# A two-layer decoder trunk with a sparse mixture of experts: the loop over overflowing expert pieces moved in front of the first expert pair, the last pair joined by one-hot products

## The chip, the cores and the metric

The kernel runs on one core of a Trainium2 chip, in one launch. The metric is device time in microseconds (us), the median of repeated executions. The profile shows one execution, taken by the hardware profiler; its engines are PE (TensorE matmul; PEld is its weight load), DVE (VectorE), ACT (ScalarE), POOL (GpSimd) and SP (SyncE, which here only issues transfers; SPq is its queue of instructions).

## The reference, cut to what matters

512 tokens of width 1024 go through two layers. In each, attention of three kinds ends in an output projection and a layer norm; then a mixture of experts (4 groups of 8 experts, each token takes its best group and that group's two best experts) and a second layer norm. All is float32.

```python
for l in range(DEPTH):                                   # DEPTH = 2
    mix = hybrid_mixer(x, ...)
    x = layer_norm(DEEPNORM_ALPHA * x + mix, ln1_g[l], ln1_b[l])
    moe = hier_moe(x, ...)
    x = layer_norm(DEEPNORM_ALPHA * x + moe, ln2_g[l], ln2_b[l])

def hier_moe(t, ...):
    lg = t @ rg_w + rg_b                                 # 4 groups, best one taken
    le = ...                                             # its 8 experts, best two taken
    gate = ...                                           # (token, group, expert), two nonzero per token
    for g in range(N_GROUPS):                            # expert: 1024 -> 2 x 256 -> 1024
        h = silu(t @ w_gate[g]) * (t @ w_up[g])
        y = y + (h * gate[:, g]) @ w_down[g]
```

## The kernel before

**The expert stage.** After the output projection, the rows of a layer are normalized without gain and bias and stored to DRAM (`xd`). A router on DVE picks two experts for each token. Every expert has 64 slots (`CAP`); two experts form a pair, so one pair is a list of 128 token rows, and there are 16 pairs for each layer. `hots` and `lists` make the lists: a one-hot matrix of slots by comparison, then a small product that gives each slot's row number and weight. `fetch` (through `gathered`, L1000) has POOL gather a pair's 128 rows from `xd`; `turned` transposes them on PE (L1011) and applies gain and bias on the way out of PSUM (L1015, L1017); `experts_up` multiplies by the gate and up weights (tile `S`); `experts_mid` makes silu times up; `experts_down` transposes that (`hT`), multiplies by the down weights (tile `o`), scales the rows on ACT (L1044) and DVE (L1045), and POOL adds the 128 rows to the sum `y2` in DRAM (L1046) by an indirect transfer that accumulates.

**The sum in DRAM.** `y2` begins as the normalized rows with gain and bias: `first_rows` makes them on DVE (L888, L889) in place, once the store to `xd` has read the tile, and ACT's queue stores them. After the last pair, SP loads `y2` back (L1251), the second norm follows (L1260 to L1265), and the result goes to `out` in the last layer, or is transposed and multiplied by the next layer's projection in the first.

**The weights.** The weights of one expert are two tiles of 1.5 MB (6144 columns in all), a pair has four, a layer 64. `load_next` issues one unit, that is two tiles, into a ring of 13 rooms: `RING = "UUAAARTTXUUmm"`, where T and m lie in the pool of the expert stage, which opens when attention's pool closes, and X in `xroom`. Six units (12 tiles) are asked for before the first pair, and each pair asks for two more, so a room is filled again once the pair that read it is done with it. SP's queue issues them in order.

**Overflow.** An expert with more than 64 tokens has the rest cut into pieces of 64. `pieces` counts them on DVE and lists them; `overflow` is a loop on the chip (`For_i`, L1139) whose number of turns every engine loads from memory (L1138). It stands behind the last pair and in front of the loads of `y2`. A turn loads the expert's two tiles whole (L1143), finds the piece's rows (L1146 to L1187), and does a small expert as above, ending in an accumulating transfer (L1209). With these inputs the first layer's loop has no turn and the second layer's has one.

**The next layer's weights.** In the first layer, the first chunk of the next projection is loaded and split into high and low parts (`load_pair`, L196, L199) behind the last pair's work, by `issue_after` on the last instruction of each engine.

Each engine works through its instructions in the order in which the tile framework's planner wrote them; only the loop's borders and the `issue_after` marks are set by hand.

## Time and profile before

| | |
|---|---|
| median of 3 runs | 1386.83 us (1380.25 to 1387.82) |
| the profiled execution | 1385.0 us, span 1383.2 us |
| PE busy | 1194.4 us (86%) |
| PE weight loads | 815.8 us (59%) |
| DVE busy | 696.6 us (50%) |
| ACT busy | 442.9 us (32%) |
| POOL busy | 292.5 us (21%) |
| HBM | 278.06 MB read, 31.82 MB written |

The shares are averages over two layers with several stages each. The span has the first layer's attention until about 380 us, its experts until about 660 us, the second layer's attention until about 1045 us and its experts until the end. For the change only the two expert stages and their borders matter, so they are read stage by stage.

### The profile page before, as it was taken

The page shows a single profiled execution, that of the slowest core. Times are in us where ns is not written, and L with a number is a line of the kernel's source. Part 1 is how long each engine was busy: PE and PEld are TensorE (multiplying, and loading weights), DVE is VectorE, ACT ScalarE, POOL GpSimd, SP SyncE. Part 2 cuts the span into 40 slices and gives each one's busy share as a digit, 9 for nine tenths or more (in the row PEclk, how much of TensorE's full clock was granted, in tenths as well). Part 3 has the DMA queues.
Part 4 walks back from the last instruction along what each step waited for, and adds up shares of the span by engine and source line. Part 5 has one row for each costly group of instructions (what it writes and reads, how often), then busy time and mean ns, then how long its engine had stood idle before and what let it go on. Part 6 is the DMA issues. An engine that isn't in the chain of part 4 may idle for free. (4 is left out here: it accounts for less than half of the span.)

```text
span 1383.2 us, 18273 instructions
## 1 busy us (share of the span) xinstructions
PE 1194.4 (86%) x6701; PEld 815.8 (59%) x6708; DVE 696.6 (50%) x1822; ACT 442.9 (32%) x1050; POOL 292.5 (21%) x286
## 2 busy tenths in 40 slices
PE   6989999999939989887599999999996699898860
PEld 6989976668924533222398899666795343332320
DVE  7599638684552422111668892668636333211125
ACT  3362256673102221111235322857611122111100
POOL 5332431201001121100332334230000122111011
PEclk9999999999969999999799999999998799999985
DMA  7321440115397999998552224200426899999943
GB/s 240 116 80 51 128 158 11 36 40 185 118 402 279 400 413 405 409 390 287 166 165 78 65 83 140 98 23 22 156 104 247 347 384 407 409 403 410 356 166 123
DMA packets 63898, 293.81 MB, mean 212 GB/s; under 512 B 16064, under 2 KB 20672, under 8 KB 48192
## 3 DMA queue, kind: packets, MB, share of 16 engines
q1 hardware_dynamic: 52128, 267.43, 50.5%
q0 software_dynamic: 9376, 16.81, 4.9%
q10 hardware_dynamic: 2304, 8.39, 1.5%
q8 instruction: 54, 0.88, 0.3%
q14 instruction: 36, 0.29, 0.1%
HBM read 278.06 MB, written 31.82 MB: 224 GB/s over the span
## 5 line engine op out<-in xcount | busy, mean ns | idle before, releaser
L97 PE MATMUL acc<-U,xh 128*128 128x384 f32 (+1 forms) x1584 | 298.9, 343 | 18.9 <-DVE xh L212 7.0
L97 PEld LDWEIGHTS acc<-U,xh 128*128 128x128 f32 x1584 | 280.5, 193 | 21.9 <-issue 6.9
L97 PE MATMUL S<-w,xg 128*64 128x512 f32 (+1 forms) x968 | 272.0, 608 | 10.6 <-DMA w<-w_e 8.9
L97 PEld LDWEIGHTS S<-w,xg 128*64 128x64 f32 x968 | 83.1, 141 | 138.8 <-issue 112.9
L1017 DVE TENSOR_SCALAR xg<-acc,lv 128x128 f32<-128x128 f32 x128 | 45.8, 404 | 179.6 <-PE S L97 142.9
L97 PE MATMUL o<-w,hT 128*64 128x512 f32 x488 | 125.4, 603 | 5.9 <-ACT hT L90 3.4
L199 POOL TENSOR_TENSOR U<-raw,U 128x768 fp32r<-128x768 f32 (+2 forms) x46 | 90.3, 1967 | 166.9 <-ACT U L196 166.9
L1046 POOL DMA_INDIRECT y<-xroom,ri x32 | 51.4, 1607 | 294.8 <-DVE xroom L1045 180.5
L1031 ACT ACTIVATE h<-S 128x256 f32<-128x256 f32 x32 | 12.3, 383 | 270.6 <-PE S L97 270.6
L196 ACT ACTIVATE U<-raw 128x768 fp32r<-128x768 f32 (+2 forms) x88 | 68.0, 812 | 71.6 <-PE acc L97 43.7
L1045 DVE TENSOR_SCALAR xroom<-o,rv 128x512 f32<-128x512 f32 x32 | 24.0, 751 | 117.7 <-PE o L97 117.7
L97 PEld LDWEIGHTS o<-w,hT 128*64 128x64 f32 x488 | 39.2, 138 | 67.1 <-issue 57.4
L1000 POOL DMA_INDIRECT xroom<-xd,ri x33 | 35.2, 1066 | 180.5 <-PE acc L1011 94.5
L199 DVE TENSOR_TENSOR U<-raw,U 128x768 fp32r<-128x768 f32 (+2 forms) x42 | 52.8, 1260 | 36.5 <-ACT U L196 34.0
L1011 PEld LDWEIGHTS acc<-cst,xroom 128*128 128x128 f32 x256 | 29.4, 147 | 60.6 <-issue 36.0
L90 ACT ACTIVATE uc<-T 128x512 f32<-128x512 f32 (+3 forms) x117 | 51.3, 460 | 40.9 <-PE T L297 39.1
L1015 ACT ACTIVATE xg<-acc,lv 128x128 f32<-128x128 f32 x128 | 48.9, 458 | 45.5 <-PE T L97 35.8
L1011 PE MATMUL acc<-cst,xroom 128*128 128x128 f32 x256 | 43.7, 298 | 22.7 <-DMA xroom<-xd,ri 20.7
L97 PE MATMUL acc<-U,oh 128*128 128x384 f32 (+1 forms) x384 | 63.3, 315 | 0.0
L1044 ACT ACTIVATE xroom<-o,rv 128x512 f32<-128x512 f32 x32 | 22.0, 687 | 111.0 <-PE o L97 111.0
L97 PEld LDWEIGHTS acc<-U,oh 128*128 128x128 f32 x384 | 56.8, 189 | 1.2 <-issue 1.0
L403 DVE MATCH_REPLACE8 uc<-m,uc 128x256 f32<-128x256 f32 (+2 forms) x96 | 51.4, 539 | 0.0
(367 smaller groups left out, 1942.0 us busy)
## 6 DMA issues: line engine op xcount, KB each, us to landing
w<-w_e SPq DMA_DIRECT2D x110, 1536.0 KB
raw<-w_in SPq DMA_DIRECT2D x64, 384.0 KB
xroom<-w_e SPq DMA_DIRECT2D x8, 1536.0 KB
w<-w_e SPq DMA_DIRECT2D x24, 512.0 KB
raw<-w_o SPq DMA_DIRECT2D x16, 384.0 KB
gb<-ln_rows SPq DMA_DIRECT2D x4, 1024.0 KB
xd<-yn ACTq DMA_DIRECT2D x8, 512.0 KB
y<-yn ACTq DMA_DIRECT2D x6, 512.0 KB
```

The lines of the kernel that those rows point to most:

```text
L90: A.activation(o, i, AF.Copy, scale=1.0 if scale is None else scale)
L97: return PE.matmul(o, l, r, start=start, stop=stop, skip_group_check=True)
L196: A.activation(hi, r, AF.Copy)
L199: e.tensor_tensor(lo, r, hi.bitcast(F32), OP.subtract)
L403: V.match_replace(out=acc_t[i][:, :n], in_to_replace=m8, in_values=acc_t[i][:, :n], imm_value=TAKEN)
L1000: G.indirect_dma_start(out=xr[0:n], out_offset=None, in_=xd, in_offset=bass.IndirectOffsetOnAxis(ap=ri[0:n], axis=0), bounds_check=S - 1, ...
L1011: PE.transpose(t[:, 128 * j:128 * j + 128], xr[:, 128 * k:128 * k + 128], ident)
L1015: A.activation(xg[:, k], o, AF.Identity, scale=lv[:, 0, k, 0:1], bias=lv[:, 0, k, 1:2])
L1017: V.tensor_scalar(xg[:, k], o, lv[:, 0, k, 0:1], lv[:, 0, k, 1:2], op0=OP.mult, op1=OP.add)
L1044: last_on["A"] = A.activation(y[:, 0:512], o[0], AF.Copy, scale=rows[1])
L1045: last_on["V"] = V.tensor_scalar(y[:, 512:1024], o[1], rows[1], None, op0=OP.mult)
L1046: return G.indirect_dma_start(out=y2, out_offset=bass.IndirectOffsetOnAxis(ap=rows[0], axis=0), in_=y, in_offset=None, bounds_check=S - 1, ...
```

## The change

- **`y2` begins at zero**, stored early in the layer from a zeroed slot of 512 columns; `first_rows` is gone. In its place each pair adds half of the normalized row with gain and bias to its own rows (each token stands in two lists): `gb1` is halved once by ACT, `half_rows` makes the row on DVE from the gathered rows, and the rows are taken out of PSUM by two `scalar_tensor_tensor` on DVE, which add it. ACT takes no part in that any more. The copy of `hT` is always DVE's.
- **Rooms.** Gathered rows and output rows are tiles of the expert stage's pool; `xroom` holds two rooms of the ring and four small rooms of 512 columns (256 KB). The ring is `UUAAARTTXXUUm`, again 13.
- **`pieces` and `overflow` stand in front of the first pair**, behind the fetch of pairs 0 and 1 and six units of weights. A turn loads its weights in 12 parts of 512 columns through the four small rooms, in front of the products that read them.
- **The last pair** is not added to `y2`. `sums` loads the second norm's gain and bias and `y2` (which then holds all other pairs) before the last pair's work; the last list's one-hot matrix is transposed (`pT`), and a product of it with the last pair's rows gives their share per token in PSUM. In the last layer a product with the identity adds `y2` in PSUM; in the first layer DVE adds it.
- **The next layer's first chunk** is loaded and split during the last pair, behind `h`, with DVE alone for the low part.

```diff
-            units = {"n": 0, "m": None}
+            units = {"n": 0, "X": 0, "m": None}
...
-                    return xroom[:, 0:UNIT]
+                    units["X"] += 1
+                    return xroom[:, UNIT * (units["X"] % 2):UNIT * (units["X"] % 2) + UNIT]
...
-            RING = "UUAAARTTXUUmm"
+            RING = "UUAAARTTXXUUm"
...
+            y2 = dr.tile([S, D], F32, name="y2", tag="y2")
+            none = ring("P")
+            G.memset(none, 0.0)
+            SP.dma_start(y2.rearrange("(p r) c -> p (r c)", r=NT).rearrange("p (n c) -> p n c", c=512), none.unsqueeze(1).to_broadcast([128, 2 * NT, 512]))
...
-            def first_rows(i):
-
-                z = yn[i] if i < NT - 1 else at.tile([128, D], F32, name="x1", tag="u", bufs=3)
-                V.tensor_tensor(z, yn[i], gb1[:, 0], OP.mult)
-                V.tensor_tensor(z, z, gb1[:, 1], OP.add)
-                A.dma_start(y2[128 * i:128 * i + 128, :], z)
-
+            A.activation(gb1.rearrange("p a d -> p (a d)"), gb1.rearrange("p a d -> p (a d)"), AF.Copy, scale=0.5)
...
-                if i:
-                    first_rows(i - 1)
...
             def row_room():
-                turns["y"] += 1
-                return carve(xroom, UNIT + 2 * D + D * (turns["y"] % 3), [D])
-
-            def gathered(ri, n=128):
-
-                xr = carve(xroom, UNIT + D * (turns["x"] % 2), [D])
-                turns["x"] += 1
+                return mo.tile([128, D], F32, name="y", tag="y", bufs=3)
+
+            def gathered(ri, n=128, tag="xr", bufs=2):
+
+                xr = mo.tile([128, D], F32, name="xr", tag=tag, bufs=bufs)
...
+            def half_rows(xr, n=128):
+
+                y = row_room()
+                V.tensor_tensor(y[0:n], xr[0:n], gb1[0:n, 0], OP.mult)
+                V.tensor_tensor(y[0:n], y[0:n], gb1[0:n, 1], OP.add)
+                return y
+
+            def next_half(p1):
+                if p1 in XR:
+                    with tc.issue_after(last_on["h"].ins):
+                        HR[p1] = half_rows(XR.pop(p1))
+                    if p1 in ahead:
+                        fetch(ahead[p1])
...
-            def experts_down(h, w, rows):
+            def experts_down(h, w, rows, y, p1):
                 hT = cp.tile([128, 2, 128], F32, name="hT", tag="rw")
-                transposes(hT.rearrange("p a b -> p (a b)"), [h[:, 0:128], h[:, 128:256]], 128)
+                transposes(hT.rearrange("p a b -> p (a b)"), [h[:, 0:128], h[:, 128:256]], 128, None, "V")
+                next_half(p1)
+                if w_next:
+                    w_next.pop()()
...
-                y = row_room()
-                last_on["A"] = A.activation(y[:, 0:512], o[0], AF.Copy, scale=rows[1])
-                last_on["V"] = V.tensor_scalar(y[:, 512:1024], o[1], rows[1], None, op0=OP.mult)
-                return G.indirect_dma_start(out=y2, out_offset=bass.IndirectOffsetOnAxis(ap=rows[0], axis=0), in_=y,
+                for n in range(2):
+                    c = slice(512 * n, 512 * n + 512)
+                    last_on["V"] = V.scalar_tensor_tensor(y[:, c], o[n], rows[1], y[:, c], op0=OP.mult, op1=OP.add)
+                return y
+
+            def added(y, ri, n=128):
+                return G.indirect_dma_start(out=y2, out_offset=bass.IndirectOffsetOnAxis(ap=ri[0:n], axis=0), in_=y[0:n],
                                             in_offset=None, bounds_check=S - 1, oob_is_err=False, compute_op=OP.add)
...
-            for p in range(2):
-                fetch(p)
-            first_rows(NT - 1)
             attn.__exit__(None, None, None)
...
-            load_next(3)
-            XG[0] = turned(XR.pop(0))
-            lists(1)
-            fetch(2)
-
+            for p in range(2):
+                fetch(p)
...
-                    w = [unit("T", "w") for _ in range(2)]
-                    for u in range(2):
-                        SP.dma_start(w[u], a["w_e"][l, bass.ds(er, 1), u].rearrange("o p f -> p (o f)"))
+                    n_part = [0]
+
+                    def part(u, c0):
+
+                        r = carve(xroom, 2 * UNIT + 512 * (n_part[0] % 4), [512])
+                        n_part[0] += 1
+                        SP.dma_start(r, a["w_e"][l, bass.ds(er, 1), u, :, c0:c0 + 512].rearrange("o p f -> p (o f)"))
+                        return r
...
                     for k in range(NK):
+                        wk = part(k // 6, 512 * (k % 6))
                         for h, c in enumerate(two):
-                            mm(gu[c, 0:FH], xg[:, k], gate_up(w, k)[:, FH * h:FH * h + FH], k == 0, k == NK - 1)
+                            mm(gu[c, 0:FH], xg[:, k], wk[:, FH * h:FH * h + FH], k == 0, k == NK - 1)
...
-            for p in range(NE // 2):
+            pieces()
+            load_next(3)
+            overflow()
+            XG[0], HR[0] = turned(XR[0]), half_rows(XR.pop(0))
+            lists(1)
+            fetch(2)
+
+            last, PL, w_next, yts = l == DEPTH - 1, NE // 2 - 1, [], []
...
+            def next_weights():
+                with tc.issue_after(last_on["h"].ins):
+                    Wc[l + 1, 0] = load_pair(w_in_src(l + 1, 0), chunks[0][1], "V")
+
+            def sums():
+
+                yus = [unit("A", "yt") for _ in range(2)]
+                for j in range(2):
+                    SP.dma_start(yus[j][:, 2 * D:3 * D], a["ln_rows"][l:l + 1, 1, j].to_broadcast([128, D]))
+                for j in range(2):
+                    yu = carve(yus[j], 0, [2, D])
+                    for i in range(2):
+                        yts.append(yu[:, i])
+                        r = 256 * j + 128 * i
+                        y2d = SP.dma_start(yu[:, i], y2[r:r + 128, :])
+                return [yu[:, 2 * D:3 * D] for yu in yus], y2d
...
+                if p == PL:
+                    gb2, y2d = sums()
...
+                elif not last:
+                    raw_room()
+                    w_next.append(next_weights)
...
+                if p == PL - 1:
+
+                    pT = mo.tile([128, NT, 128], F32, name="pT", tag="xr", bufs=2)
+                    transposes(pT.rearrange("p a b -> p (a b)"), [Pf[:, i, 128:256].bitcast(F32) for i in range(NT)], 128)
...
+                if p != PL:
+                    sts[p] = added(y, rows[0])
...
-            overflow()
...
+            for i in range(NT):
+                zb[i] = [bank(("acc", "S", "o")[i % 3]) for _ in halves]
+                for t, c in zip(zb[i], halves):
+                    if last:
+                        mm(t, ident, yts[i][:, c], True, False)
+                    mm(t, pT[:, i], y[:, c], not last, True)
...
-                src = [z[:, c] for c in halves]
+                src = [z[:, c] for c in halves] if not last else zb[i]
+                if not last:
+                    for t, c in zip(zb[i], halves):
+                        V.tensor_tensor(z[:, c], z[:, c], t, OP.add)
```

## Rows read from the trace of the kernel before

**Rows 1.** The chain that ended last, 1205 to 1317: start, us, what

```profile
1205.24 35.27 DMA w<-w_e
```

**Rows 2.** Windows, first layer: length, engines' busy us (instructions), PE clock, DMA share, GB/s

```profile
376.00:412.00 36.00, 15.03 (x94) 11.22 (x94) 21.55 (x87) 2.93 (x4) 3.34 (x3) 0.69 1.01 399
412.00:428.00 16.00, 13.79 (x58) 6.45 (x58) 5.43 (x23) 4.59 (x10) 1.99 (x2) 0.74 0.44 158
440.00:600.00 160.00, 145.00 (x659) 59.84 (x661) 44.99 (x159) 30.09 (x74) 29.61 (x23) 0.98 1.02 408
```

**Rows 3.** The same windows, second layer

```profile
1076.00:1092.00 16.00, 7.15 (x30) 5.79 (x32) 7.58 (x43) 2.30 (x5) 3.55 (x3) 0.50 1.02 431
1092.00:1100.00 8.00, 7.93 (x40) 2.96 (x38) 1.52 (x5) 1.30 (x4) 0.20 (x1) 0.96 0.44 139
1100.00:1317.00 217.00, 197.45 (x884) 73.79 (x880) 54.76 (x181) 39.15 (x96) 37.07 (x28) 0.98 1.00 395
```

**Rows 4.** Timeline of SP: the first weights into rooms that pair 0 freed

```profile
423.83 0.80 SPq L530 DMA_DIRECT2D w<-w_e  x2
...
1096.81 0.80 SPq L530 DMA_DIRECT2D w<-w_e  x2
```

**Rows 5.** Timeline: a first row that waits for its store, and pair 0's gather, both layers

```profile
387.66 1.23 DVE L888 TENSOR_TENSOR yn<-yn,gb 128x1024 f32<-128x1024 f32 x1 [4.74 <-DMA xd<-yn]
403.73 1.78 POOL L1000 DMA_INDIRECT xroom<-xd,ri  x1 [21.48 <-DVE ri L986]
...
1067.73 1.22 DVE L888 TENSOR_TENSOR yn<-yn,gb 128x1024 f32<-128x1024 f32 x1 [5.30 <-DMA xd<-yn]
1077.57 1.54 POOL L1000 DMA_INDIRECT xroom<-xd,ri  x1 [22.16 <-DVE ri L986]
```

**Rows 6.** Timeline of PE: pair 0's gathered rows turned, first up products

```profile
414.14 1.97 PE L1011 MATMUL acc<-cst,xroom 128*128 128x128 f32 x8 [6.67 <-DMA xroom<-xd,ri]
416.68 8.83 PE L97 MATMUL S<-w,xg 128*64 128x512 f32 x32
...
1090.22 8.29 PE L97 MATMUL S<-w,xg 128*64 128x512 f32 x32
```

**Rows 7.** Timeline of DVE: first and last of the 17 instructions of `pieces`

```profile
1138.33 0.38 DVE L1117 TENSOR_TENSOR over<-cnt,cst 128x224 f32<-128x224 f32 x1
...
1144.01 0.16 DVE L1132 TENSOR_SCALAR eidi<-eid 128x16 int32<-128x16 f32 x1
```

**Rows 8.** Timeline of the loop's one turn in the second layer

```profile
1329.85 0.23 DVE L1146 TENSOR_SCALAR h<-cst,ctr 128x16 f32<-128x16 f32 x1 [0.42 <-DVE xroom L1045]
1340.88 5.81 PE L97 MATMUL S<-w,xg 128*64 128x256 f32 x32 [1.51 <-DVE xg L1189]
1352.21 1.44 POOL L1209 DMA_INDIRECT y<-xroom,ri  x1 [15.64 <-DVE xroom L1208]
```

**Rows 9.** Tiles `xroom` and `y`, second layer's expert stage: issue to landing

```profile
DMA to landing us min/median/max: 2.6/10.1/12.0
...
DMA to landing us min/median/max: 9.1/11.2/12.0
```

**Rows 10.** Waits of SP around the loop in the first layer: us, times, longest

```profile
SPq L1139 <- DMA y<-xroom,ri: 11.2, 1, 11.2
```

**Rows 11.** Timeline: last pair's end and first statistics of the second norm, both layers

```profile
655.63 3.71 PE L97 MATMUL o<-w,hT 128*64 128x512 f32 x16 [0.56 <-issue]
668.92 0.06 DVE L1134 MEMSET ctr<- 128x1 f32 x1 [3.60 <-issue]
671.69 0.69 DVE L1260 BATCH_NORM_STATS2 bst<-yt 128x6 f32<-128x512 f32 x1 [2.71 <-DMA yt<-y]
...
1323.47 5.17 PE L97 MATMUL o<-w,hT 128*64 128x512 f32 x16 [0.52 <-ACT hT L90]
1328.68 0.75 DVE L1045 TENSOR_SCALAR xroom<-o,rv 128x512 f32<-128x512 f32 x1 [6.22 <-PE o L97]
1359.57 0.69 DVE L1260 BATCH_NORM_STATS2 bst<-yt 128x6 f32<-128x512 f32 x1 [7.63 <-DMA yt<-y]
```

More of the change, by code (lines that the diff above doesn't have):

```diff
@@ L956, in trunk @@
             V.tensor_scalar(hot, hot, TAKEN, None, op0=OP.is_equal)
-            selb = small.tile([128, NT, 8, 4], BF, name="selb", tag="selb", bufs=1)
+            selb = small.tile([128, NT, 8, 4], BF, name="selb", tag="stN", bufs=1)
             gb = ghot.unsqueeze(2).to_broadcast([128, NT, 8, 4])
@@ L1216, in trunk @@
                 h = experts_mid(gu)
-                if p + 1 < NE // 2:
-                    XG[p + 1] = turned(XR.pop(p + 1))
-                    fetch(p + 3)
-                if p % 2 == 0 and p // 2 + 2 < NE // 4:
-                    lists(p // 2 + 2)
-                st = experts_down(h, w, RI.pop(p))
-                load_next()
-                if p % 2:
-                    tc.declare_no_dep(st.ins, st0.ins, reason="a token has one group: the two pairs of a batch share no row")
-                st0 = st
-                if p == 3:
-                    pieces()
-                    gb2 = norm_rows(1)
-            last = l == DEPTH - 1
-            with tc.issue_after(last_on["PE"].ins), tc.issue_after(last_on["A"].ins), tc.issue_after(last_on["V"].ins), tc.issue_after(st.ins):
-                if not last:
-                    raw_room()
-                    Wc[l + 1, 0] = load_pair(w_in_src(l + 1, 0), chunks[0][1], "VG")
-            overflow()
+                if p != PL:
+                    p1 = ORDER[q + 1]
+                    with tc.issue_after(last_on["up"].ins):
+                        XG[p1] = turned(XR[p1])
+                elif not last:
+                    raw_room()
+                    w_next.append(next_weights)
+                if q + 4 < n:
+                    p4 = ORDER[q + 4]
+                    if p4 % 2 == 0:
+                        Pf = lists(p4 // 2)
+                if p == PL - 1:
+                    pT = mo.tile([128, NT, 128], F32, name="pT", tag="xr", bufs=2)
+                    transposes(pT.rearrange("p a b -> p (a b)"), [Pf[:, i, 128:256].bitcast(F32) for i in range(NT)], 128)
+                rows = RI.pop(p)
+                y = experts_down(h, w, rows, HR.pop(p), ORDER[q + 1] if p != PL else None)
+                load_next()
+                if p != PL:
+                    sts[p] = added(y, rows[0])
+                    if p < PL and p % 2:
+                        tc.declare_no_dep(sts[p].ins, sts[p - 1].ins, reason="a token has one group: the two pairs of a batch share no row")
             if not last:
-                warm(10)
                 XH[l + 1] = xhp.tile([128, 2, NK, S], F32R, name="xh", tag="xh")
@@ L1243, in trunk @@
             halves = [slice(0, 512), slice(512, 1024)]
-            yts = []
-            for j in range(2):
-                yu = carve(unit("A", "yt"), 0, [2, D])
-                for i in range(2):
-                    yts.append(yu[:, i])
-                    r = 256 * j + 128 * i
-                    for c in halves if r == 0 else [slice(0, 1024)]:
-                        y2d = SP.dma_start(yu[:, i, c], y2[r:r + 128, c])
-            if not last:
-                with tc.issue_after(y2d.ins):
-                    Wc[l + 1, 1] = load_pair(w_in_src(l + 1, 1), chunks[1][1], "VG")
+            zb = {}
+            for i in range(NT):
[4 more added lines that the diff above has]
+                    mm(t, pT[:, i], y[:, c], not last, True)
             for i in range(NT):
                 z = yts[i]
-                src = [z[:, c] for c in halves]
+                src = [z[:, c] for c in halves] if not last else zb[i]
+                if not last:
+                    for t, c in zip(zb[i], halves):
+                        V.tensor_tensor(z[:, c], z[:, c], t, OP.add)
                 st = small.tile([128, 2, 6], F32, name="bst", tag="bst", bufs=4)
```

49 lines of the change are left out of this document (27 added, 22 removed).

## The prediction

> **What bounds the kernel now.** I read the chain of waits first. In the second layer's expert stage it is a run of weight loads, four links from 1205 to 1317, the first of 35.27 us [rows 1]. The windows by stage say the same of both layers: the DMA share is 1.02 from 440 to 600 and 1.00 from 1100 to 1317, at some 400 GB/s [rows 2, 3]. So the expert stage ends when its transfers have gone through, and only time in which the transfers rest can be won or lost. They rest once in each layer, at the start: share 0.44 for 16 us (9.0 us idle) and 0.44 for 8 us (4.5 us) [rows 2, 3]. There all free rooms are filled, and SP waits for pair 0 to free the first: the refills at 423.83 and 1096.81 [rows 4] come 7.2 and 6.6 us after pair 0's first up product at 416.68 and 1090.22 [rows 6]. From there the transfers do not stop until the last pair. This is the rule for the sum: each microsecond by which pair 0 begins sooner or later moves the end of its layer's expert stage by one, and work on PE or DVE inside the stage costs nothing as long as it hides under the loads.
>
> What follows the last weights is bare: in the first layer 12.4 us from the last down product's end (655.63 + 3.71) to the first statistics at 671.69; in the second 30.9 us, from 1328.64 to 1359.57, with the loop's one turn in it [rows 11].
>
> **First layer, front.** The first rows go. DVE waited 4.74 us for the store to `xd` and then had four such instructions of 1.22 us between the router's own [rows 5], 9.6 us. Pair 0's gather moves from 403.73 to about 394, and with the 10.4 us that it took to reach PE [rows 5, 6] it lands at about 404.5. New in between: `pieces`, 17 instructions over 5.8 us [rows 7], behind the lists at about 395, so until 401; then the loop with no turn. What that costs shows at its old place: DVE stood 3.60 us before its next instruction at 668.92 [rows 11], and SP had waited 11.2 us there for a transfer [rows 10], so I read the exit as a meeting of all engines that also waits for transfers in flight. 401 + 3.6 gives 404.6. The weights asked for before would be in by about then: the transfers were full to 412 [rows 2] with one tile of 1.5 MB and 2 MB of first-row stores that now fall away, 3.5 MB at 399 GB/s, 9 us. So the loop ends at 406 to 408; PE needs 2.5 us from the first transposes to the first up product [rows 6], which then comes at 408.5 to 410.5. I take the later: 6 us won. Bounds: 9 if the loop is hidden by the gather; 3 if the jump takes as long as a gather under full load, 10.1 us [rows 9], ending at 411.
>
> A page of the Trainium skill speaks for the lower bound: Runtime: NRT & Kernel Launch, section Instruction fetch mechanics, says that a taken branch to a target outside the two blocks held makes the sequencer fetch it by DMA before it goes on. The trace agrees in that engines stand at the exit; no row separates fetch from meeting. By that rule the jump competes with full weight queues and the term is 3, not 6.
>
> **First layer, end.** The 12.4 us hold extraction, the accumulating transfer, the loop's exit and the load of `y2`. In their place: two extractions by DVE, 0.75 us each as its old one [rows 11]; two products of 512 columns (sixteen half-width ones took 3.71 us [rows 11], so 0.2 to 0.9 each, I take 0.9); two additions, 0.75 each as the extraction: 4.8 us. Then the split of the next layer's weights: it lay in the hidden wait, and that cover is gone. Four subtractions on DVE, at most 1.23 each [rows 5], either stand ahead of the extraction (and wait for their load, which SP issues only behind the reads of `y2`) or follow it: 0 to 5 us, I take 2.5. Won: 12.4 − 4.8 − 2.5 = 5, bounds 3 and 8.
>
> **Second layer, front.** Without the first rows DVE saves 5.30 + 4 × 1.22 = 10.2 us; but the gather needs the store to `xd`, which landed at 1067.73 [rows 5]: it starts at 1068, not 1077.57, and the lists are done at about 1068.5. `pieces` ends at 1074, the loop begins at about 1075 with room for a first move. Its turn took 22.4 us from first DVE work to its last transfer (1329.85 to 1352.21), 1.4 to issue that [rows 8] and 2.6 at least to land [rows 9]: 26.4. New in it: weights by parts. The up products took 5.81 us for eight parts' worth [rows 8], 0.73 a part; four parts are there at the start, the fifth is asked for after the first is read and is in 2.6 us later [rows 9], 0.4 late, and the four for the down product likewise. I take 3 us, bounds 1 and 6 (landing at 5). PE starts it at clock 0.50 [rows 3], having stood: I take 2, bounds 0 and 5.8, all up products at half speed. Extraction by DVE alone and the half rows have DVE idle beside them. Exit 1.5, bounds 1 and 3.6. So 1075 + 26.4 + 3 + 2 + 1.5 = 1108, first up product 2.5 later, 1110.4: 20 us lost. Bounds 14 and 30. The thirteenth tile (3.8 us at 408 GB/s) fits between exit and first refill.
>
> **Second layer, end.** The turn and the load of `y2` leave the tail. After 1328.64: 1.5 us extraction, 0.9 to 1.8 product (the identity product needs only `y2` and can go first). `y2` itself waits for the adding of pair 14, median 11.2 us to land [rows 9]; pairs come about 15 us apart at the end (four tiles of 3.8), so it lands near the last product's end and the read 2.6 later. I take 4 us to the first statistics, bounds 3 and 8: 27 won, bounds 23 and 28. The norm starts with a whole row at once, not halves: 0.5, bounds 0 and 1.5.
>
> **Inside the stage.** DVE gets 2 × 1.22 for half a row, 0.75 more extraction and each `hT`: some 3.4 us a pair, 51 on 54.76 busy of 217 [rows 3]. Cover: the weight loads; price if it fails, in the rivals. The zeroing of `y2` and ACT's halving lie under attention and the output projection, where transfers and ACT have room; nothing if so.
>
> **Sum**, against the profiled execution's 1385.0 (span 1383.2): 6 + 5 − 20 + 27 + 0.5 = 18.5 won, 1366.5. The median lies 1.8 above that execution: **1368 us**. All bad ends give 3 + 3 − 30 + 23 + 0 = −1, so 1388; all good ones 9 + 8 − 14 + 28 + 1.5 = 32.5, so 1354.
>
> **Rivals.**
> *The jump pays for its fetch* (the rule above): 3 us less in the first layer and the exit at 3.6 in the second: 1373. For it: 3.60 us idle; against: the second layer's exit lay between 1352.21 and 1359.57 with transfer and load inside.
> *The read of `y2` still gates the end*: POOL adds pair 14 late because it works in order behind the adding before; the read lands 8 us after the last product in both layers, so 23 and 1 instead of 27 and 5: 1376. For it: the 11.2 us landings; against: 15 us a pair.
> *DVE becomes a link of each pair, slower than before*: the two `o` banks are free only after the extraction, and that may stand behind the half rows. PE had 197.45 busy of 217 [rows 3], some 1.4 us of room in each of 14.5 pairs. If all 3.4 us enter the chain, 2.0 a pair over 28 pairs is 56: 1424. It decides from about 0.9 us a pair beyond the room. Against: between two down products lie up products of 8 us.
> *Parts one at a time, slower too*: if the rooms work as one, 12 × (2.6 + 0.73) = 40 us for 11 in my sum: 1397. Against: `xroom` already held gathered rows, output rows and weights at the same time. A rule of the Trainium skill (DMA: Bandwidth & Descriptors, section Bandwidth: batch transfers to at least 1 MiB) speaks against parts; no row shows a load that small.
> *Better than 1354*: the loop hides more than its bounds say.
>
> **How the numbers follow.** Chances: forecast 0.55 (own range 1357 to 1379), jump 0.14, `y2` 0.12, DVE 0.07, parts 0.06, better 0.06. The range 1354 to 1386 holds the first three nearly whole and leaves 0.18 out. A measurement here tells 0.5% (6.9 us) from no change. Faster: 0.51 + 0.13 + 0.09 + 0.06 = 0.79; same: 0.04 + 0.01 + 0.03 + 0.01 = 0.09; slower: 0.07 + 0.05 = 0.12.
>
> **What would show it.** In the changed kernel's profile: pair 0's gather some 10 us earlier in both layers; first up products at about 411 and 20 us later than before in the second layer; transfers resting there for some 30 us after 1080; share near 1.0 afterwards; statistics some 4 us behind the last down product. It is wrong if the share inside the stage falls below 0.95 (DVE rival), if the turn takes 45 us (parts), or if the idle at the loop is much longer than these numbers.

## The result, and the profile after

The changed kernel takes 1369.89 us (median of 4 runs, 1367.66 to 1371.29), the kernel before 1386.34: ratio 0.9893, 95% interval 0.9863 to 0.9923. The forecast was 1368. The profiled execution takes 1368.62 us, with a span of 1366.8.

The time falls into nine stages whose borders are rows of the timelines: the router's first group maximum (DVE, 382.76 and 1055.92 before, 382.99 and 1047.68 after), the first weights into rooms that pair 0 freed (SP, [rows 4] before), the end of the last pair's down product (PE) and the first statistics of the second norm (DVE, both [rows 11] before).

| stage | before | after | difference | foreseen |
|---|---|---|---|---|
| 1 start to the first layer's router | 382.8 | 383.0 | +0.2 | 0 |
| 2 router to first refill, first layer | 41.1 | 34.9 | -6.2 | -6 |
| 3 first refill to last down product | 235.5 | 239.8 | **+4.3** | 0 |
| 4 last down product to statistics | 12.4 | 3.2 | -9.2 | -5, with stage 5 |
| 5 statistics to the second layer's router | 384.2 | 386.8 | +2.6 | |
| 6 router to first refill, second layer | 40.9 | 58.4 | +17.5 | +20 |
| 7 first refill to last down product | 231.8 | 235.2 | **+3.4** | 0 |
| 8 last down product to statistics | 30.9 | 3.8 | -27.1 | -27 |
| 9 statistics to the end | 23.6 | 21.7 | -1.9 | -0.5 |
| span | 1383.2 | 1366.8 | -16.4 | -18.5 |

The timeline of the changed kernel at the first layer's front (start, us, engine, line, operation, idle before and what ended it), which answers to [rows 4 to 7]:

```profile
395.61 1.26 POOL L994 DMA_INDIRECT xr<-xd,ri  x1 [13.29 <-DVE eidi L1143]
395.91 0.17 DVE L1142 TENSOR_SCALAR eidi<-eid 128x16 int32<-128x16 f32 x1
408.52 1.23 DVE L1017 TENSOR_TENSOR y<-xr,gb 128x1024 f32<-128x1024 f32 x1 [12.43 <-issue]
410.76 2.46 PE L97 MATMUL S<-w,xg 128*64 128x512 f32 x6
417.88 1.14 SPq L532 DMA_DIRECT2D w<-w_e  x2
```

The gather starts 8 us earlier than before. `pieces` cost little: its instructions ran between those of the lists, the last at 395.91, and the gather began 1.6 us later than the forecast's 394; no run leaves `pieces` out. All engines then stand in the loop without a turn for 12 us, DVE from 396.1 to 408.52. The transfers have run dry by 407 (DMA share 0.00 from 407 to 408), and 1.3 us later the engines go on.

The second layer's front, timeline, with the loop's one turn (it answers to [rows 8], and the last row to [rows 4]):

```profile
1061.25 0.23 DVE L1162 TENSOR_SCALAR h<-cst,ctr 128x16 f32<-128x16 f32 x1 [0.66 <-DVE eidi L1142]
1066.82 0.94 POOL L994 DMA_INDIRECT xr<-xd,ri  x1 [4.32 <-DVE ri L984]
1073.37 1.22 DVE L1017 TENSOR_TENSOR y<-xr,gb 64x1024 f32<-64x1024 f32 x1 [7.34 <-DMA xr<-xd,ri]
1077.02 2.40 PE L97 MATMUL S<-xroom,xg 128*64 128x256 f32 x10 [2.51 <-DVE xg L1205]
1086.01 2.71 PE L97 MATMUL o<-xroom,hT 128*64 128x512 f32 x8 [0.37 <-ACT hT L90]
1090.55 1.47 POOL L1226 DMA_INDIRECT y<-y,ri  x1 [22.79 <-DVE y L1225]
...
1106.04 1.14 SPq L532 DMA_DIRECT2D w<-w_e  x2
```

Windows of both layers, columns as in [rows 2] (then PE clock, DMA share, GB/s):

```profile
404.00:418.00 14.00, 9.36 (x40) 4.85 (x42) 7.54 (x25) 4.07 (x6) 1.32 (x1) 0.72 0.42 152
440.00:600.00 160.00, 138.56 (x642) 60.26 (x638) 70.27 (x163) 18.90 (x50) 30.72 (x22) 0.97 1.02 408
1072.00:1092.00 20.00, 10.45 (x50) 4.29 (x50) 5.51 (x7) 0.65 (x2) 1.45 (x1) 0.76 0.37 120
1092.00:1104.00 12.00, 8.41 (x30) 4.22 (x32) 5.91 (x18) 4.08 (x6) 0.02 (x1) 0.61 0.40 135
1104.00:1320.00 216.00, 193.65 (x884) 84.07 (x880) 97.20 (x229) 26.46 (x70) 40.44 (x28) 0.96 0.97 385
```

In the turn the transfers rest for more than half of 32 us, where [rows 3] had 8 us at 0.44. DVE in the loads' stage went from 44.99 to 70.27 us of 160.

The first layer's end, timeline ([rows 11] before):

```profile
652.09 5.61 PE L97 MATMUL o<-w,hT 128*64 128x512 f32 x16 [0.77 <-DMA w<-w_e]
652.15 1.75 SPq L1252 DMA_DIRECT2D yt<-y  x4
654.50 4.07 SPq L194 DMA_DIRECT2D raw<-w_in  x4
660.89 0.69 DVE L1306 BATCH_NORM_STATS2 bst<-yt 128x6 f32<-128x512 f32 x1
664.21 0.75 ACT L196 ACTIVATE U<-raw 128x656 fp32r<-128x656 f32 x1 [13.83 <-DMA raw<-w_in]
666.14 1.32 PE L1321 MATMUL T<-cst,yt 128*128 128x128 f32 x8 [1.32 <-DVE yt L1311]
681.06 1.94 PE L1321 MATMUL T<-cst,yt 128*128 128x128 f32 x8 [13.59 <-DVE yt L1311]
682.65 0.62 PE L97 MATMUL acc<-U,xh 128*128 128x328 f32 x1
```

The statistics start 9.2 us sooner after the last product, but the next layer's first projection product starts at 682.65, 2.9 us later than before (679.73). From the last down product (its end is 657.70 here, 659.34 before) to that product it takes 25.0 us, before 20.4: PE turned row 0 at 666.14 and then stood 13.6 us for row 1.

The second layer's loads and end, chain of waits (start, us, what; it answers to [rows 1]):

```profile
1166.60 32.97 DMA w<-w_e
...
1327.72 8.88 DMA y<-y,ri
1336.61 6.44 DMA yt<-y
1343.10 3.71 PE acc L97 x8
```

Again four links of weights, to 1304, then pair 14's adding and the read. The timeline of the same end:

```profile
1336.13 5.14 PE L97 MATMUL o<-w,hT 128*64 128x512 f32 x16 [0.52 <-DVE hT L92]
1345.12 0.70 DVE L1306 BATCH_NORM_STATS2 bst<-acc 128x6 f32<-128x512 f32 x1 [3.07 <-PE acc L97]
```

The read of `y2` lands at 1343.05, 1.8 us after the last down product (1341.27); the statistics start at 1345.12.

### The profile page after: what moved, and what is told of

Same layout as the page of the kernel before. It is cut to its first block, busy times and chain, and to the rows that moved or that the text cites. A ratio compares the mean times of both kernels' runs of the same rounds, so it can differ in the third digit from the quotient of the medians.

```text
span 1366.8 us, 18439 instructions
## 1 busy us (share of the span) xinstructions
PE 1206.3 (88%) x6754; PEld 835.6 (61%) x6754; DVE 791.6 (58%) x1932; ACT 424.6 (31%) x1007; POOL 293.6 (21%) x284
## 5 line engine op out<-in xcount | busy, mean ns | idle before, releaser
L97 PE MATMUL acc<-U,xh 128*128 128x384 f32 (+1 forms) x1584 | 299.0, 343 | 16.4 <-DVE xh L212 7.2
L97 PE MATMUL S<-w,xg 128*64 128x512 f32 x848 | 241.8, 612 | 37.0 <-DMA w<-w_e 30.9
L1042 DVE TENSOR_TENSOR h<-h,S 128x256 f32<-128x256 f32 x32 | 13.5, 421 | 172.5 <-ACT h L1041 172.5
L994 POOL DMA_INDIRECT xr<-xd,ri x33 | 42.6, 1289 | 272.9 <-issue 106.4
L1062 POOL DMA_INDIRECT y<-y,ri x30 | 47.5, 1585 | 153.8 <-DVE y L1058 153.8
L97 PE MATMUL S<-xroom,xg 128*64 128x512 f32 (+1 forms) x208 | 68.6, 600 | 12.3 <-DMA xroom<-w_e 7.5
L1058 DVE SCALAR_TENSOR_TENSOR y<-o,rv,y 128x512 f32<-128x512 f32 x64 | 47.9, 750 | 53.6 <-PE o L97 49.7
L199 DVE TENSOR_TENSOR U<-raw,U 128x768 fp32r<-128x768 f32 (+2 forms) x44 | 56.0, 1277 | 35.0 <-ACT U L196 32.1
L1005 PEld LDWEIGHTS acc<-cst,xr 128*128 128x128 f32 x256 | 31.5, 156 | 50.4 <-issue 50.4
L1005 PE MATMUL acc<-cst,xr 128*128 128x128 f32 x256 | 39.9, 306 | 21.6 <-issue 21.6
L1017 DVE TENSOR_TENSOR y<-xr,gb 128x1024 f32<-128x1024 f32 (+1 forms) x33 | 40.2, 1217 | 24.8 <-issue 17.5
```

Of the source, the lines that this page charges most:

```text
L97: return PE.matmul(o, l, r, start=start, stop=stop, skip_group_check=True)
L199: e.tensor_tensor(lo, r, hi.bitcast(F32), OP.subtract)
L994: G.indirect_dma_start(out=xr[0:n], out_offset=None, in_=xd, in_offset=bass.IndirectOffsetOnAxis(ap=ri[0:n], axis=0), bounds_check=S - 1, ...
L1005: PE.transpose(t[:, 128 * j:128 * j + 128], xr[:, 128 * k:128 * k + 128], ident)
L1017: V.tensor_tensor(y[0:n], xr[0:n], gb1[0:n, 0], OP.mult)
L1042: last_on["h"] = V.tensor_tensor(h, h, gu[:, FH:2 * FH], OP.mult)
```

## The experiments

Ratios are against the kernel before, run beside it on the same chip. Stages are those of the table, in profiled executions.

**The loop's price at either place.** Two kernels without the loop:

```diff
             load_next(3)
-            overflow()
             XG[0], HR[0] = turned(XR[0]), half_rows(XR.pop(0))
```

> The changed kernel without the loop over overflowing pieces, in both layers; the second layer's one piece is left out. Theory (the loop in front is paid for in full, because all thirteen rooms are full of weights and none comes free until the first pair has run): from the router's first result to the first refill takes 32 us in both layers, in place of 34.9 and 59.1, and the loads' stages keep their 240 and 234.5 us; 1338 to 1345 us in all. Rival (the stand in front is partly made good later, because the rooms are full and the arithmetic catches up): the loads' stages get longer by as much as the front gets shorter, and no more than 12 us are won, 1357 us or more.

```diff
                 Wc[l + 1, 0] = load_pair(w_in_src(l + 1, 0), chunks[0][1], "VG")
-            overflow()
```

> The kernel before without the loop over overflowing pieces, in both layers; the second layer's one piece is left out. Theory (at the end, too, a turn is paid for in full): from the last down product to the first statistics takes 5 to 7 us in the second layer in place of 30.9, and 8 to 10 in the first in place of 12.35; 1355 to 1361 us. Rival (the read of the sums, not the turn, sets most of that end): 1370 us or more. With the first experiment this gives the price of the loop at either place: by the theory 27 us in front and 27 to 30 at the end, so that moving it alone wins almost nothing, and what the change won comes from the last pair's one-hot join.

Measured: the changed kernel without the loop 1343.09 us, ratio 0.9708 (0.9691 to 0.9726); the one before without it 1354.26, ratio 0.9788 (0.9771 to 0.9805). The first theory holds in time and stages; by the second the ends were to be shorter than they are (9.0 and 10.9 us against 5 to 7 and 8 to 10), and the time is 0.7 us below its range, but its rival of 1370 falls. The refills of the changed kernel without the loop, timeline of SP:

```profile
413.56 0.80 SPq L532 DMA_DIRECT2D w<-w_e  x2
...
1079.10 0.80 SPq L532 DMA_DIRECT2D w<-w_e  x2
```

Router to refill takes 30.7 and 31.4 us in place of 34.9 and 58.4: in front the loop costs 4.2 + 27.0 = 31.2. At the end it costs 1.5 (12.4 against 10.9) and 21.9 (30.9 against 9.0), 23.4 in all. By spans the two prices are 27.2 and 31.4. Most of the difference lies in stage 5, which went opposite ways in the two pairs (392.5 without the loop in front, 374.9 without the one at the end), partly by the clock: what its falls cost in the four executions (last section) leaves 30.6 and 24.6 of the two prices. Without the loop in front the loads' stages kept their length within 1.6 us (238.2 and 234.4), so what is lost in front does not come back. So the loop, in its new place and with its weights in parts, costs 6 to 8 us more than in the old. What won is the rest of the change, 12.2 us of span between the two kernels without a loop: 10.6 and 10.3 in the fronts, where the first rows are gone, and 7.4 and 5.1 behind the last down products; it lost 2.5 in each loads' stage and 17.6 in stage 5, 5.1 of that by the clock.

**Why the loads' stages got longer.** The slices 8 to 16 us behind the first refill, windows, of the kernel before and of the changed one, first layer then second:

```profile
431.83:439.83 8.00, 8.00 (x42) 3.27 (x39) 1.64 (x4) 1.28 (x3) 1.67 (x2) 1.00 0.90 343
1104.81:1112.81 8.00, 8.00 (x42) 3.25 (x39) 1.63 (x4) 1.28 (x3) 1.65 (x2) 1.00 0.90 335
```

```profile
425.88:433.88 8.00, 8.00 (x36) 2.43 (x32) 3.51 (x7) 0.00 (x0) 3.15 (x2) 1.00 0.60 201
1114.04:1122.04 8.00, 8.00 (x36) 2.43 (x32) 3.51 (x7) 0.00 (x0) 3.15 (x2) 1.00 0.65 220
```

About 1 MB less comes through there, and the runs without the loop in front, without the late rows and with row 0's early product have 0.63 to 0.65 there as well (the run with an empty turn, below, 0.84 and 0.76). The second refill, whose rooms the first down product frees, comes 12.7 us behind the first in both layers, before 9.6. Three kernels ask what does it. The first leaves out the half rows:

```diff
-                        HR[p1] = half_rows(XR.pop(p1))
+                        XR.pop(p1)
+                        HR[p1] = row_room()
...
-                    last_on["V"] = V.scalar_tensor_tensor(y[:, c], o[n], rows[1], y[:, c], op0=OP.mult, op1=OP.add)
+                    last_on["V"] = V.tensor_scalar(y[:, c], o[n], rows[1], None, op0=OP.mult)
```

> The changed kernel without the two VectorE operations a pair that put the first normalisation's rows into the expert's rows (their share of the sum is left out; the result of the down product is only scaled). Theory A (VectorE's added work delays the copy that the first down product waits for, so the second refill comes late): the slice 8 to 16 us behind the first refill goes from a DMA share of 0.60 and 0.64 back to 0.85 to 0.90, and the loads' stages lose 1.5 to 2.5 us each; 1364 to 1367 us. Theory B (the megabyte of gains and biases that now stands at the stage's end costs the time): the stages stay at 240 and 234.5 us, 1369 us. Theory C (VectorE has become the pace of the stage): they lose more than 5 us each, under 1360 us.

Measured: 1344.21 us, which cannot be compared, because other values reach the second layer's router, no expert overflows there and the turn falls away. Its stages can: 236.9 and 233.1 in place of 239.8 and 235.2, and the slices at 0.71 and 0.72, short of the 0.85 that theory A asks for. Theory A is right in kind; it explains 2.9 and 2.1 us. C falls. The second:

```diff
                 yus = [unit("A", "yt") for _ in range(2)]
-                for j in range(2):
-                    SP.dma_start(yus[j][:, 2 * D:3 * D], a["ln_rows"][l:l + 1, 1, j].to_broadcast([128, D]))
...
-                return [yu[:, 2 * D:3 * D] for yu in yus], y2d
+                return [gb1[:, j] for j in range(2)], y2d
```

> The changed kernel without the load of the second normalisation's gain and bias rows (1 MB a layer) at the end of the stage; the first normalisation's rows, halved, stand in for them, so the result is scaled differently. Theory B (that megabyte stands ahead of the last weights' landing): the loads' stages lose 2 to 2.6 us each, 1364 to 1366 us, and the last down product of the first layer takes 3.7 us in place of 5.6. Theory A (only VectorE's delay at the start counts): no change, 1368 to 1371 us.

Measured: 1367.80, ratio 0.9883 (0.9866 to 0.99); stages 239.0 and 237.0. Theory B falls: the megabyte at the end costs nothing that can be seen. The third keeps all work and takes it off DVE for one pair:

```diff
-            def half_rows(xr, n=128):
+            def half_rows(xr, n=128, e=V):
...
-                        HR[p1] = half_rows(XR.pop(p1))
+                        HR[p1] = half_rows(XR.pop(p1), e=G if p1 == ORDER[1] else V)
...
-                transposes(hT.rearrange("p a b -> p (a b)"), [h[:, 0:128], h[:, 128:256]], 128, None, "V")
+                transposes(hT.rearrange("p a b -> p (a b)"), [h[:, 0:128], h[:, 128:256]], 128, None, "A" if p1 == ORDER[1] else "V")
```

> The changed kernel with the second pair's first rows made by GpSimd and the first pair's hidden copies turned by ScalarE, both in place of VectorE, and nothing else moved: only VectorE's queue behind the first pair gets shorter. Theory A (that queue holds the first pair's down product, and so the second refill, back): the slice 8 to 16 us behind the first refill goes from a DMA share of 0.60 and 0.64 to 0.80 to 0.90 and the loads' stages lose 1.5 to 2.5 us each; 1364 to 1367 us. Rival (the order that TensorE's instructions were put in holds it, or GpSimd's slower operations delay the next gather): the slice stays under 0.7, 1368 to 1373 us.

Measured: 1370.17, ratio 0.9904 (0.9881 to 0.9926): no gain. The slices:

```profile
427.56:435.56 8.00, 8.00 (x36) 2.43 (x32) 1.50 (x2) 0.00 (x0) 1.62 (x1) 1.00 0.81 302
1116.98:1124.98 8.00, 8.00 (x36) 2.43 (x32) 1.50 (x2) 0.00 (x0) 1.63 (x1) 1.00 0.83 317
```

Theory A again: the share is back at 0.81 and 0.83, and the stages take 237.4 and 233.1. But the stages in front took 37.8 and 62.0 in place of 34.9 and 58.4. The timeline there shows a part of why, and below it the same comparison in the changed kernel, alone:

```profile
407.45 3.23 POOL L1017 TENSOR_TENSOR y<-xr,gb 128x1024 f32<-128x1024 f32 x1 [10.51 <-issue]
408.39 2.57 DVE L1070 TENSOR_TENSOR oneh<-posm,cst 128x256 fp32r<-128x256 f32 x1
```

```profile
409.67 0.42 DVE L1070 TENSOR_TENSOR oneh<-posm,cst 128x256 fp32r<-128x256 f32 x1
```

The planner put GpSimd's two operations beside pair 0's own work. The DVE instruction that takes 0.42 us there took 2.57 and ended at 410.96, 0.3 us behind GpSimd's (410.68). What the stages won (2.4 and 2.1), the fronts lost (2.9 and 3.6), so the time is that of the rival.

**The first layer's end.** Two kernels ask why PE stood 13.6 us. One issues the next weights ahead of the reads of `y2`:

```diff
-                    gb2, y2d = sums()
+                    yus = sums()
...
                 y = experts_down(h, w, rows, HR.pop(p), ORDER[q + 1] if p != PL else None)
+                if p == PL:
+                    gb2, y2d = sum_reads(yus)
```

(`sum_reads` holds the four loads of `y2`, `sums` the rest.)

> The changed kernel with the loads of the second layer's first projection weights ahead of the reads of the sums in SyncE's queue (both still behind the last experts' weights). Theory (VectorE's split of these weights stands ahead of the normalisation of token rows 1 to 3 and waits for a load that is queued behind 2 MB of reads): the gap of 13.6 us in TensorE between the transposes of row 0 and of row 1 shrinks under 5, and from the last down product of the first layer to the first projection product it takes 14 to 19 us in place of 25.0; 1359 to 1364 us. Rival (the reads of the sums come as much later as the weights come earlier, so the first statistics start later): 22 to 25 us, 1367 to 1371.

Measured: 1367.85, ratio 0.9884 (0.9858 to 0.991), no different from the change. From the last down product to the first projection product it took 25.3 us. The weights were split by 661.5, but the statistics came at 662.61, 6.5 us behind the product in place of 3.2, and row 1 was turned at 679.61. The theory falls. The rival is nearer (25.3 against 22 to 25): the reads came later, and VectorE's work on row 1 is late either way. The other gives PE something to do while it stands:

```diff
                 if i == 0:
+                    early = bank("acc")
+                    c = slice(0, 128)
+                    mm3(early[:, :328], lambda k: XH[l + 1][:, 0, k, c], lambda k: XH[l + 1][:, 1, k, c], Wc[l + 1, 0], 0, 328)
...
-                    project(0, i, d0, tag)
+                    if i:
+                        project(0, i, d0, tag)
+                    else:
+                        evac(early, i, d0)
```

> The changed kernel with token row 0's product with the second layer's first projection weights traced ahead of the transposes of rows 1 to 3 (row 3's joined sums use other banks), so that TensorE has it to do in the 13.6 us in which it stands for row 1. Theory (TensorE stands there only because row 1's transposes come first in its order, and is the pace from there on): the 5.4 us of row 0's product run from about 671, the projection is done 4 to 6 us sooner and with it the second layer's router; 1362 to 1366 us. Rival (VectorE's work on rows 1 to 3 is the pace until about 690, so TensorE waits for it later instead): 1368 to 1371 us.

Measured: **1359.81**, ratio 0.983 (0.9804 to 0.9856). Stage 5 takes 378.0 in place of 386.8, more than foreseen. Timeline of PE:

```profile
667.57 0.56 PE L97 MATMUL acc<-U,xh 128*128 128x328 f32 x2
...
675.98 4.79 PE L97 MATMUL acc<-U,xh 128*128 128x384 f32 x17 [0.82 <-POOL U L199]
681.51 1.06 PE L1324 MATMUL T<-cst,yt 128*128 128x128 f32 x8 [0.74 <-DVE yt L1314]
```

Both of row 0's projection products, the 384 columns too, moved into the gap. DVE's work on row 1 is as late as before; PE no longer waits for it with work at hand. The clock has no part in this: its falls cost 1.7 us in this execution as in the changed kernel's (last section).

**Other places for the loop.** Three kernels put it between pairs, with the parts issued by ACT or by SP:

```diff
-            overflow()
...
             for q, p in enumerate(ORDER):
+                if q == 2:
+                    overflow()
...
-                        SP.dma_start(r, a["w_e"][l, bass.ds(er, 1), u, :, c0:c0 + 512].rearrange("o p f -> p (o f)"))
+                        A.dma_start(r, a["w_e"][l, bass.ds(er, 1), u, :, c0:c0 + 512].rearrange("o p f -> p (o f)"))
```

> The changed kernel with the loop moved from ahead of the first pair to ahead of the third, the parts of the piece's weights issued by ScalarE and so in another queue than the experts' weights; the piece's rows are made in place. Theory (a turn costs little where refills are queued to run during it): from the router's first result to the first refill 31 us in both layers, as without a loop, and the loads' stages get longer by the piece's own 3 MB and a little more, 8 to 14 us in the second layer and 0 to 4 in the first; 1346 to 1354 us. Rival (the loop's two meetings wait for the transfers in flight, so the rooms stand as before): the stages get longer by 20 us or more in the second layer and by 8 or more in the first; 1362 to 1375.

> The same move of the loop to ahead of the third pair, with the parts left in SyncE's queue behind the refills. If the place alone counts: as the run with the parts in ScalarE's queue, within 3 us. If the order in the queue counts: the first part lands only when the refills ahead of it have (up to 6 units, some 20 us at 400 GB/s), the turn is longer by that, and while the rest of the piece runs no refill is queued: 5 to 15 us above that run.

> The same with the loop ahead of the fifth pair, parts in ScalarE's queue. If the stand is hidden by the refills that are queued when it begins: the same as ahead of the third pair or up to 5 us less, since by then more rooms are empty. If the meeting waits for all transfers in flight: up to 10 us more, since more of them are.

Measured: 1381.09 (ratio 0.998, 0.997 to 0.999), 1376.62 (0.9948, 0.9931 to 0.9964) and 1374.20 (0.993, 0.991 to 0.9949): none better than in front. The first two are clearly worse; the third lies within the noise of the ratios (0.9893 in front), and its four stages take 572.6 us together against 568.3. The fronts took 30.3 to 30.8 us, as without a loop, but the stages 250.0 and 269.7, 249.7 and 267.0, 248.4 and 263.1. The first layer: the timeline of the run ahead of the third pair (ACT's queue), then two windows of the run ahead of the fifth:

```profile
451.21 0.06 DVE L1144 MEMSET ctr<- 128x1 f32 x1 [15.72 <-SPq L1149]
```

```profile
460.00:480.00 20.00, 0.00 (x0) 0.00 (x0) 0.00 (x0) 0.00 (x0) 0.56 (x1) 0.55 0.99 400
480.00:485.00 5.00, 0.94 (x4) 0.32 (x6) 1.08 (x5) 0.00 (x0) 0.00 (x0) 0.50 0.15 63
```

Without a turn, all engines stand in the loop until the queued weights have landed, 15.7 us ahead of the third pair and some 22 ahead of the fifth; then every room is full, and the transfers rest until pairs have run. The first run's rival holds in kind (10 and 35 us longer stages), though the time is 6 us above its range. Of the other two forecasts none came true: with the parts in SP's queue it was 4.5 us faster, not slower or the same, and ahead of the fifth pair 6.9 us faster, a little more than the most that either theory allowed.

**An empty turn.** The count of pieces is set to none:

```diff
-                V.tensor_copy(eidi[:, MAX_ITEMS:], end[:, NE - 1:NE])
+                V.memset(eidi[:, MAX_ITEMS:], 0)
```

> The changed kernel with the count of overflowing pieces set to none in both layers: the loop and its meeting stay, the second layer's one piece is left out. If the meeting is what costs in front: the second layer's first refill comes 50 us or more behind the router's first result, and 1360 us or more. If the turn costs and the empty meeting is nearly hidden behind the gather: 33 to 37 us, as in the first layer (34.9), and 1345 to 1350 us, 3 to 5 above the run without a loop.

Measured: **1330.74**, ratio 0.9615 (0.9587 to 0.9643), 12 us less than without a loop (0.9708), which no theory had. Router to refill: 27.4 and 29.8, 3.3 and 1.6 less than without a loop. So the meeting need not cost anything in front, and the turn, with the wait for its count, costs 58.4 - 29.8 = 28.6; with the real count the empty loop costs 4.2 (34.9 against 30.7). The kernels differ in one more thing: here the count is known from the start, so SP enters the loop at 382, and two tiles of weights (3 MB) wait behind it. The gathers' median to landing was 6.7 us in this run and 10.5 in the changed kernel (DMA issues in the window 392 to 404 of the one, 392 to 405 of the other):

```profile
xr<-xd,ri POOLq DMA_INDIRECT x2, 6.7
```

```profile
xr<-xd,ri POOLq DMA_INDIRECT x2, 10.5
```

DVE's longest wait in the loop was 2.3 us in place of 10.3 (instructions of the loop's line on DVE's queue, ns min/median/max, first and last start in us):

```profile
L1149 DVEq EVENT_SEMAPHORE  x24: 21/50/2327, 396.4 to 1058.5; - x24
```

```profile
L1149 DVEq EVENT_SEMAPHORE  x23: 21/50/10343, 396.7 to 1095.0; - x23
```

**The same with the real count**, on top of row 0's early product:

```diff
-            RING = "UUAAARTTXXUUm"
+            RING = "UUAAARTTUUXXm"
...
-            load_next(3)
+            load_next(3 if l else 2)
             overflow()
+            if l == 0:
+                load_next(1)
```

> The kernel with row 0's projection product ahead, and in the first layer the last two units of the rooms' first filling (3 MB, the third pair's second half, now in the two big rooms) loaded behind the loop in place of ahead of it. Theory (the first pair's gather lands late because it shares the DMA engines with those units, and the empty loop is left only when all in flight has landed): in the first layer the gather lands 3 to 5 us sooner, the first up product starts 23 us behind the router's first result in place of 27.8, the weights flow from about 402 on, and the last down product ends at 650 to 653 in place of 657.7; 1352 to 1356 us. Rival (what is loaded later is missing later, or the gather takes its 10 us whatever else flows): the last down product ends at 656 or later; 1358 to 1362 us.

Measured: **1356.93**, ratio 0.9802 (0.9773 to 0.9832), the fastest with the piece in it; its interval overlaps that of the run before it, but the stages show the gain. The first layer, DMA issues in the window 392 to 405, then the timeline:

```profile
xr<-xd,ri POOLq DMA_INDIRECT x2, 4.5
```

```profile
401.55 0.82 SPq L535 DMA_DIRECT2D xroom<-w_e  x2
403.89 1.98 PE L97 MATMUL S<-w,xg 128*64 128x512 f32 x4
```

The gather lands in 4.5 us (10.5 in the run before it), the weights flow from 401.55, the first up product starts 21.6 us behind the router's first result (27.9), the last down product ends at 652.36 (657.79). The theory holds: the gather gains more than its 3 to 5 us, the first up product comes sooner than its 23, and only the total lies outside, 0.9 us above its range.

## Why the prediction was right, and where it was not

The time came out 1.9 us above the forecast, and that it came so near is in part luck. The two fronts and the second layer's end were right or nearly so; 7.7 us were lost inside the stages, where the forecast had nothing, and most of that was made good by some 5 us of clock that no term held and by a turn that began sooner than foreseen.

*First layer, front (6 foreseen, 6.2 measured).* The steps were met: gather at 395.61 (about 394), loop's end at 408.3 (406 to 408), first up product at 410.76 (408.5 to 410.5). The exit does wait for transfers in flight. Not foreseen: with two tiles fewer in flight the same loop is left 6.4 us sooner, counted from the router's first result. Against the jump rival: 10.3 of DVE's 12.4 us were one wait for a semaphore, and its branches of the loop took at most 0.08 us each; a stand of some 22 us (ahead of the fifth pair) is also longer than any gather took to land in [rows 9]. In the 1.3 us between the last transfer and the next work no row separates a fetch from the meeting.

*Second layer, end (27 foreseen, 27.1 measured).* Right. The rival by which the read of `y2` gates the end is half there: the read landed 1.8 us behind the last product, but inside the 4 us.

*Second layer, front (20 lost foreseen, 17.5 measured).* The turn, from its first DVE work to the engines' return at 1095.0, took 33.8 us against the 33 of my sum. The start was mis-sized: the forecast put `pieces` behind the lists and the turn 19 us after the router's first result; the turn began 13.6 after it, since the planner laid the instructions of the two between each other. Part of that was lost again: pair 0's up product frees its room 8.3 us after it starts (6.6 before), in a window at granted clock 0.61.

*First layer, end (5 foreseen).* Stage 4 won 9.2 and stage 5 gave 2.6 back, 6.6 in all; without the clock's part in stage 5 (5.0, below) 1.6 are left, so the number was met by luck. The failed step is "0 to 5 us, I take 2.5" for the split: it counted DVE's instructions, not that PE's order holds row 1's transposes ahead of row 0's projection. PE stood 13.6 us, and the run with row 0's product first had 8.8 of stage 5 back.

*Inside the stage (0 foreseen, 7.7 lost).* This step failed: "From there the transfers do not stop until the last pair", and with it "work on PE or DVE inside the stage costs nothing". The second has a condition, that the work hides under the loads, and the forecast took it as met. It is met from 16 us after the first refill on (share 1.01 to 1.03). Before that, one late down product holds back the second refill, and DVE's longer queue made it late: the refill came 3.1 us later behind the first than before, and 1.4 and 1.5 later with less in that queue (first layer; the first pair relieved, no half rows). The rival in which DVE becomes a link was priced for all pairs, and it was only the first. The same two runs have 4.5 and 5.0 us of the 7.7 back; the rest is open.

*Norm (0.5 foreseen, 1.9 measured)*: mis-sized, not looked into. *Parts one at a time*: the up product took 7.35 us (1077.02 to 1084.37) for 5.81, so no.

Of the span's 16.4 us, some 5 are the clock's: without them the same sum is about 11.4, inside the range and 7 short of the 18.5.

## What to carry to other kernels

A loop whose count is read on the chip was left, in these runs, only when every queued transfer had landed: put it where little is queued and nothing waits for a room, and ask what must land before it, not only how long a turn takes. Price such a loop at either place by leaving it out: here the loop's new place cost more than the old one, and the rest of the change won the time. "Hidden under the loads" is a statement about the steady state; at a stage's start, where all rooms are full, one late instruction on an engine that is busy for 44% of the stage thins out the transfers (share 0.60 for 8 us). Where an engine stands for a late operand, look at what lies behind in its own order: here moving a product won more than making the operand earlier.

## What the chip showed that was not expected

- DVE and GpSimd hindered each other: the 128x256 comparison took 2.57 us beside a GpSimd operation and 0.42 alone. The Trainium skill, SBUF — State Buffer, section SBUF: two separate sides, says that the two share a port pair which one holds for a whole instruction while the other is blocked, on DVE's side for instructions with two inputs in SBUF among others; this one has two. The trace agrees: DVE's ended 0.3 us behind GpSimd's.
- The same gather of 128 rows landed in 10.5 us beside full weight queues and in 4.5 with two tiles (3 MB) fewer ahead of it.
- The granted clock of PE in the second layer's attention differs between executions of almost the same work. Windows of the kernel before, of the changed one, and of the one before without the loop (columns as in [rows 2]):

```profile
760.00:780.00 20.00, 16.55 (x81) 15.74 (x80) 17.43 (x45) 8.11 (x23) 9.31 (x9) 0.83 0.27 80
880.00:900.00 20.00, 16.88 (x107) 12.57 (x107) 15.95 (x52) 16.64 (x61) 2.34 (x1) 0.83 0.05 5
```

```profile
760.00:780.00 20.00, 16.91 (x90) 15.79 (x89) 17.97 (x48) 8.32 (x23) 9.42 (x9) 0.91 0.55 183
```

```profile
760.00:780.00 20.00, 16.93 (x102) 15.78 (x101) 18.82 (x50) 8.23 (x22) 9.41 (x9) 1.00 0.25 79
```

PE is at the lower of its two levels (1.2 GHz, shown as 0.50) for a part of such a window. At 0.83, 20 us do 3.4 us less work, at 0.91 1.8; before had two of the first kind (6.8), the changed kernel one of the second, a difference of 5.0. Summed over windows of 1 us from 700 to 1030 the falls cost 6.8 us before, 1.7 in the changed kernel, 5.1 and nothing in the two without the loop (in front, at the end), and 1.7 in both with row 0's early product. PE had been busy at 1.00 and then stood just before each fall shown, 3.45 and 2.45 us before, 3.09 in the changed kernel; but it stood 3.07 us at the first place in the run without the loop too, where the clock did not fall. So a stand goes ahead of a fall and does not decide it; what does was not tried.
